# A Strassen-type MLP on one core: product sums kept across passes, and a quarter of the other two column blocks taken the same way

## The chip, the cores and the metric

One Trainium2 chip, one core of it. The metric is device time of one launch in microseconds (us); the kernel before takes 2032.7 us in the median of three runs (2032.12 to 2035.39). The engines named below are TensorE (PE in the profile, with PEld for its weight loads), VectorE (DVE), ScalarE (ACT), GpSimd (POOL) and SyncE (SP), whose queue issues nearly all transfers.

## The reference, cut to what matters

A decoder trunk of two layers over 256 tokens, model width 2048, hidden width 8192, in float32. Layer 0 mixes with a gated short convolution, layer 1 with multi-head latent attention; both end in the same kind of MLP, and the change is in the MLP.

```python
def sq_relu_mlp(x, w1, w2):
    return jnp.square(jax.nn.relu(x @ w1)) @ w2

for layer in range(DEPTH):
    ...
    h = layer_norm(ALPHA * h + mix, ln_g[layer, 0], ln_b[layer, 0])
    h = layer_norm(ALPHA * h + sq_relu_mlp(h, mlp_w1[layer], mlp_w2[layer]),
                   ln_g[layer, 1], ln_b[layer, 1])
```

## The kernel before, in words

**Precision.** TensorE multiplies operands of type float32r. To come near float32, every operand is split into a high part `hi` (a ScalarE cast, L116) and a low part `lo` (a VectorE subtraction, L117), and each product is made of three: hi·hi, hi·lo, lo·hi. So each weight tile of 128x1024 that arrives costs one cast of ScalarE and one subtraction of VectorE before TensorE can use it. `stream` (from L69) lists all weight tiles of 512 KB in the order in which TensorE wants them; `take` (L166) hands out the next and has later ones prepared, `LOOK` = 5 tiles ahead. Raw tiles have `RAW` = 5 buffers, split tiles `WA` = 8. Instructions are placed on their engines by a scheduler ahead of time, which may move an instruction of an engine before an earlier one that is not ready; on the chip each engine keeps its fixed order.

**The MLP** (`mlp`, L557) runs in `NQ` = 8 passes over the hidden width. A pass makes 8 tiles of 128 hidden units by 256 tokens (`products`, L265: 16 steps of one 512-wide and one 256-wide matmul each; `hidden`, L593: evacuation, ReLU, square, split into `h`), then multiplies them with the 1024 rows of W2 that belong to them, onto `acc`, 256 tokens by 2048, held in SBUF as 2 token tiles `t` by `NB` = 4 column blocks `n` of 512.

- `down` (L288), the plain way, takes one column block: 4 weight tiles, each of 2 K tiles by 512 columns, give 4 x 2 x 2 `dot`s. A `dot` (L274) is three matmuls with a 512-wide moving operand. That is 48 matmuls for a block.
- `down_fast` (L316), used in the six passes of `FAST` (1 to 6), takes blocks 0 and 1 together by a Strassen-Winograd step: 2 token tiles by 2 K tiles by 2 column blocks need 7 dots instead of 8, so 4 pairs of K tiles give 84 matmuls instead of 96. It needs seven PSUM banks ("4", "2", "3", "1", "6", "7", "5", in that order, `FACTORS` L313), sums of hidden tiles (`forms`, L602 to L609) and sums of weights, which `prepare` (L137 to L160) makes from two raw tiles: a difference of 1024 (L149), two of 512 (L152, L155), three splits of 1024 (`lo` twice, `lo_t`) and one of 512 (`t`, the operand "T4" of the first dot). The code counts such a unit as three tiles.
- `combine` (L642) adds the seven sums of a pass into `acc` right after: 11 additions of 128x512 on VectorE and one copy on ScalarE (L649), with a scratch `vu` from the pool of raw tiles. Blocks 2 and 3 then go through `down`, with four more additions.
- In the second MLP, `turn_residual` (L903) transposes the residual of one column block on TensorE and adds it to `acc`, in each of passes 1 to 4, between blocks 2 and 3.
- Pass 0 and pass 7 take all four blocks the plain way; pass 7 hands over to the norm behind it (`to_wide` L658, `to_out` L911). `to_out` loads gain and bias, `gbt`, on POOL's queue (L914).

**PSUM** has 8 banks, in two pools of four; `psum` (L180) counts its calls, and `Banks.next` (L106) gives calls 0 to 3 of each eight to one pool and 4 to 7 to the other.

Of the kernel before, what the change touches and what calls it, by code (L numbers as in the profile page):

```python
# [36 lines left out]
FAST = range(1, NQ - 1)  # L37
FIRST = (0, 1, 2, 4, 6, 8, 12, 16)
# [12 lines left out]
def trunk(ctx: ExitStack, tc: tile.TileContext, xT, vecs, w_first, w_in, w_out, w_kv, w_q, w_uk, w_uv,  # L51
          w_qn, w_qp, w_o, w1, w2, w2f, cosT, sinT, mask, ident, gb, out):
# [258 lines left out]


# [3 lines left out]
    def down_fast(x, forms):  # L316

        ps = {p: psum(f"ps_f{p}") for p, _, _ in FACTORS}
        n = len(x) // 2
        for j in range(n):  # L320
            b, = take(1)
            a = {"11": held(x[2 * j], 0), "12": held(x[2 * j + 1], 0), "22": held(x[2 * j + 1], 1)}
            for i in range(4):
                a[f"S{i + 1}"] = [forms[:, j, o, i * P:(i + 1) * P] for o in range(2)]
            for p, l, r in FACTORS:
                dot(ps[p], b[r], a[l], j == 0, j == n - 1)
        return ps
# [14 lines left out]
    cos_t = const.tile([P, T], F32, name="cos_t")  # L342
    sin_t = const.tile([P, T], F32, name="sin_t")
    mask_t = const.tile([P, 3 * P], F32, name="mask_t")
# [9 lines left out]

    def late_constants():
        nc.sync.dma_start(id_t, ident)
        nc.sync.dma_start(cos_t, cosT)
        nc.sync.dma_start(sin_t, sinT)
        nc.sync.dma_start(mask_t, mask)
# [193 lines left out]
    late_constants()  # L553
# [3 lines left out]
    def mlp(idx, ln, blocks, fast, begin=None, extra=None):  # L557
# [24 lines left out]

        for q in range(NQ):
# [8 lines left out]

            def hidden(m, ps, evac, *func):  # L593
                f = tmp.tile([P, T], F32, tag="fh", name="fh", bufs=3)
                evac(ps, f, *func)
                if not func:
                    nc.scalar.activation(f, f, AF.Relu)  # L597
                nc.scalar.activation(f, f, AF.Square)
                put_split(h[m], f)
                pair.append(f)  # L600
                if forms is not None and m % 2:
                    (a11, a21), (a12, a22) = ((v[:, :P], v[:, P:]) for v in pair[-2:])  # L602
# [39 lines left out]
    def combine(put, p):  # L642

        put(0, 1, p["4"])
        put(0, 0, p["2"])
        put(1, 0, p["3"])
        v, u = (raws.tile([P, 2, BW], F32, tag="raw", name="vu")[:, i, :] for i in range(2))
        put(0, 0, p["1"])
        nc.scalar.copy(v, p["1"])  # L649
        nc.vector.tensor_tensor(v, v, p["6"], ALU.add)  # L650
        nc.vector.tensor_tensor(u, v, p["7"], ALU.add)
        put(1, 0, v)
        put(0, 1, u)
        put(1, 0, p["5"])
        put(1, 1, u)
        put(1, 1, p["5"])
# [31 lines left out]
    with tc.tile_pool(name="att", bufs=1) as ap:  # L688
        lat = act.tile([P, 2 * NK, 2 * T], F32R, tag="c", name="lat")
        chl, qhl = ([lat[:, k, :] for k in range(o, o + NK)] for o in (0, NK))  # L690
        kpe = ap.tile([P, 2, T], F32, name="kpe")
# [6 lines left out]
        def rope(dst, src, rows):  # L698

            a = tmp.tile([P, T], F32, tag="sq", name="ropea")  # L700
            b = tmp.tile([P, T], F32, tag="nu", name="ropeb")
# [201 lines left out]
    def turn_residual(block, n):  # L903
        if 0 <= n < NB:
            for t in range(2):
                ps = psum("turned")
                for j in range(4):
                    nc.tensor.transpose(ps[:, j * P:(j + 1) * P], xres[:, 4 * n + j, t * P:(t + 1) * P], id_t)
                nc.vector.scalar_tensor_tensor(block(n, t), ps, ALPHA, block(n, t), ALU.mult, ALU.add)

    def to_out(block, put, h):  # L911
        gbt = act.tile([P, NB, 2 * BW], F32, tag="b", name="gbt")
        for n in range(NB):
            nc.gpsimd.dma_start(gbt[:, n, :], gb[n].partition_broadcast(P))  # L914
# [148 lines left out]
```

## Time and profile before

| | before |
|---|---|
| median of 3 runs | 2032.7 us (2032.12 to 2035.39) |
| the profiled execution: its time, its span | 2031.86 us, 2030.0 us |
| granted TensorE clock | 1.000 |
| busy: PE, PEld, DVE, ACT | 2022.8, 1763.4, 1637.1, 1186.2 us |
| the six passes of `FAST` in the first MLP | 455.4 to 970.1 us, 85.8 us each |
| in the second MLP | 1413.9 to 1932.2 us, 86.7 us each in passes 1 to 4, 85.8 us in 5 and 6 |

The profile is one execution. "PE" are matmuls, and as they are pipelined the duration of one is longer than the time from its start to the next one's; a cost per matmul is therefore read from starts. "Idle before" an instruction is time in which its engine did nothing, and the name behind the arrow is what ended it.

### The profile page before, as it was taken

To read this page: it belongs to the slowest core of one execution; us is meant where nothing else is said; L and a number is where in the kernel's file an instruction comes from. 1 tells how busy PE (TensorE), PEld (TensorE's weight loads), DVE (VectorE), ACT (ScalarE), POOL (GpSimd) and SP (SyncE) were. 2 spreads that over 40 slices of the span, in tenths; PEclk is the share of its full clock that TensorE was granted. 3 is DMA by queue.
4 is the path that set the end of the run, shared out by engine and by line. 5 is a ranking of instruction groups with operands and counts; after the bars stand their busy time and mean duration, and the time that the engine had idled before them with its cause. 6 is when DMAs were issued, how large, how long until landed. Compare 5 with 4: busy or idle time off the path is not lost.

```text
span 2030.0 us, 30192 instructions
## 1 busy us (share of the span) xinstructions
PE 2022.8 (100%) x11240; PEld 1763.4 (87%) x11240; DVE 1637.1 (81%) x2559; ACT 1186.2 (58%) x1849; POOL 4.5 (0%) x25
## 2 busy tenths in 40 slices
PE   9999999999999999999999999999999999999998
PEld 8888888988888888888889998898888888888886
DVE  7667677778898988989788978776889898898966
ACT  6444445676566565655656655566656656565661
POOL 0000000000000000000000000000000000000000
PEclk9999999999999999999999999999999999999999
DMA  8666666564746557465654544656474664746573
GB/s 307 209 191 187 188 190 193 162 210 138 251 148 216 193 170 256 145 229 174 232 176 153 177 129 137 195 168 205 136 240 155 213 204 164 250 143 221 190 228 121
DMA packets 106851, 385.32 MB, mean 190 GB/s; under 512 B 11856, under 2 KB 12752, under 8 KB 106448
## 3 DMA queue, kind: packets, MB, share of 16 engines
q1 hardware_dynamic: 105984, 381.17, 57.9%
q0 software_dynamic: 576, 2.10, 0.3%
q8 instruction: 88, 1.44, 0.3%
q14 instruction: 59, 0.48, 0.1%
q10 hardware_dynamic: 144, 0.13, 0.0%
HBM read 381.25 MB, written 2.10 MB: 189 GB/s over the span
## 4 chain that ended last, share of the span: by engine, by line
PE 99%; DMA 0%; DVE 0%; issue 0%; SPq 0%; ACT 0%; DVEq 0%
PE ps_u L192 20%; PE ps_l L192 13%; PE ps_u L196 11%; PE ps_d L276 7%; PE ps_d L277 7%; PE ps_d L278 7%; PE ps_l L196 7%; PE ps_f L278 4%; PE ps_f L276 4%; PE ps_f L277 4%; PE ps_w L226 1%; PE ps_w L224 1%; PE ps_w L225 1%; PE ps_g L226 1%; PE ps_g L224 1%; PE ps_g L225 1%
## 5 line engine op out<-in xcount | busy, mean ns | idle before, releaser
L117 DVE TENSOR_TENSOR lo<-raw,hi 128x1024 fp32r<-128x1024 f32 x710 | 858.7, 1222 | 271.5 <-ACT hi L116 199.9
L116 ACT CAST hi<-raw 128x1024 fp32r<-128x1024 f32 x710 | 740.9, 1050 | 428.4 <-DMA raw<-in_w_dram 134.6
L192 PE MATMUL ps_u<-xhl,hi 128*128 128x512 f32 x1792 | 621.3, 391 | 0.0
L196 PE MATMUL ps_u<-xhl,lo 128*128 128x256 f32 x1792 | 500.1, 280 | 0.0
L192 PEld LDWEIGHTS ps_u<-xhl,hi 128*128 128x128 f32 x1792 | 334.4, 187 | 71.9
L196 PEld LDWEIGHTS ps_u<-xhl,lo 128*128 128x128 f32 x1792 | 339.2, 189 | 1.7
L276 PE MATMUL ps_d<-hi,h 128*128 128x512 f32 x640 | 249.9, 390 | 0.0
L277 PE MATMUL ps_d<-lo,h 128*128 128x512 f32 x640 | 249.3, 390 | 0.0
L278 PE MATMUL ps_d<-hi,h 128*128 128x512 f32 x640 | 249.2, 389 | 0.0
L192 PE MATMUL ps_l<-xhl_a,hi 128*128 128x512 f32 x704 | 244.1, 393 | 0.0
L196 PE MATMUL ps_l<-xhl_a,lo 128*128 128x256 f32 x704 | 195.5, 280 | 0.0
L192 PEld LDWEIGHTS ps_l<-xhl_a,hi 128*128 128x128 f32 x704 | 132.2, 188 | 29.8
L278 PEld LDWEIGHTS ps_d<-hi,h 128*128 128x128 f32 x640 | 120.2, 188 | 25.2
L276 PEld LDWEIGHTS ps_d<-hi,h 128*128 128x128 f32 x640 | 120.2, 188 | 25.0
L277 PEld LDWEIGHTS ps_d<-lo,h 128*128 128x128 f32 x640 | 120.2, 188 | 24.6
L196 PEld LDWEIGHTS ps_l<-xhl_a,lo 128*128 128x128 f32 x704 | 131.9, 188 | 0.2
L597 ACT ACTIVATE fh<-fh 128x256 f32<-128x256 f32 x112 | 46.5, 415 | 89.2 <-DVE fh L333 89.1
L116 ACT CAST hi_t<-raw_t 128x1024 fp32r<-128x1024 f32 x48 | 50.6, 1054 | 55.5 <-DVE raw_t L149 30.5
L192 PE MATMUL ps_l<-z,hi 128*128 128x512 f32 x240 | 82.4, 391 | 0.0
L226 PE MATMUL ps_w<-xd,hi 128*128 128x258 f32 x256 | 72.7, 285 | 0.0
L224 PE MATMUL ps_w<-xd,hi 128*128 128x258 f32 x256 | 72.6, 284 | 0.0
L225 PE MATMUL ps_w<-xd,lo 128*128 128x258 f32 x256 | 72.4, 283 | 0.0
(253 smaller groups left out, 3185.1 us busy)
## 6 DMA issues: line engine op xcount, KB each, us to landing
raw<-in_w_dram SPq DMA_DIRECT2D x416, 512.0 KB, 4.3
raw<-in_w2f_dram SPq DMA_DIRECT2D x96, 512.0 KB, 3.5
raw<-in_w_in_dram SPq DMA_DIRECT2D x88, 512.0 KB, 3.8
raw<-in_w_out_dram SPq DMA_DIRECT2D x32, 512.0 KB, 3.6
raw<-in_w_o_dram SPq DMA_DIRECT2D x32, 512.0 KB, 4.0
raw<-in_w_kv_dram SPq DMA_DIRECT2D x10, 512.0 KB, 3.6
raw<-in_w_q_dram SPq DMA_DIRECT2D x8, 512.0 KB, 4.4
raw<-in_w_uk_dram SPq DMA_DIRECT2D x8, 512.0 KB, 4.6
```

The costliest lines, as they stand in the source:

```text
L116: nc.scalar.copy(hi, src)
L117: nc.vector.tensor_tensor(lo, src, hi.bitcast(F32), ALU.subtract)
L192: nc.tensor.matmul(ps, w[blk // 8][0][:, blk % 8, :], x, start=first, stop=False)
L196: nc.tensor.matmul(ps[:, :T], w[blk // 8][1][:, blk % 8, :], x[:, :T], start=False, stop=last)
L224: nc.tensor.matmul(ps[:, :W], hi, x[k][:, :W], start=k == 0, stop=False)
L225: nc.tensor.matmul(ps[:, :W], lo, x[k][:, :W], start=False, stop=False)
L226: nc.tensor.matmul(ps[:, :W], hi, x[k][:, W:], start=False, stop=k == NC - 1)
L276: nc.tensor.matmul(ps, x[0], w[0], start=first, stop=False)
L277: nc.tensor.matmul(ps, x[0], w[1], start=False, stop=False)
L278: nc.tensor.matmul(ps, x[1], w[0], start=False, stop=last)
L597: nc.scalar.activation(f, f, AF.Relu)
```

## The change

Four things in the MLP, and some moves that make room for them in SBUF.

1. `combine` goes. The seven sums of a pass are added to running sums (`keep`): "2", "3", "4", which go to one place each, straight to `acc`; "1", "6", "7", "5" to `sums`, 16 KB a partition. In pass 1 the first visit to `sums` is a copy on ScalarE.
2. `fold` brings `sums` into `acc` once an MLP, eight additions of 128x1024 on VectorE, one after each hidden tile of pass 7.
3. Blocks 2 and 3 are taken together (`down_pairs`). Three of the four pairs of K tiles are multiplied the plain way, onto four banks named "22", "3", "2", "4"; the fourth goes through the seven dots, of which "4", "2", "3" continue on the banks of that name and "1", "6", "7", "5" get new ones. `turn_residual` is called twice with one token tile each.
4. `hidden` works on two tiles of a pair in one buffer, and splits both with one cast and one subtraction of 128x512.
5. Room: `cos_t`, `sin_t`, `mask_t` are loaded at the start of the attention; `ropeb` shares a buffer; `gbt` is loaded on SP's queue, and the scratch of POOL's queue is cut to 4096.

```diff
+PLAIN = QC // 2 - 1
...
-            lead = 0
-            if q in FAST:
-                out += [(w2f[l, q, j, 0], w2f[l, q, j, 1]) for j in range(QC // 2)]
-                lead = 2
-            out += halves(w2[l, q, lead:])
+            if q not in FAST:
+                out += halves(w2[l, q])
+                continue
+            out += [(w2f[l, q, j, 0], w2f[l, q, j, 1]) for j in range(QC // 2)]
+            for j in range(PLAIN):
+                out += halves(w2[l, q, 3, j]) + halves(w2[l, q, 2, j])
+            out += [(w2g[l, q, j, 0], w2g[l, q, j, 1]) for j in range(QC // 2 - PLAIN)]
...
-    def down_fast(x, forms):
-
-        ps = {p: psum(f"ps_f{p}") for p, _, _ in FACTORS}
-        n = len(x) // 2
-        for j in range(n):
-            b, = take(1)
...
-                dot(ps[p], b[r], a[l], j == 0, j == n - 1)
-        return ps
+    OWN = ("1", "6", "7", "5")
+    def fast_products(ps, x, forms, j, fresh, last):
+
+        b, = take(1)
...
+            dot(ps[p], b[r], a[l], p in fresh, last)
...
+        sums = fast.tile([P, 4, 2, BW], F32, name=f"sums{idx}")
+
+        def keep(p, g, ps):
+
+            at = sums[:, OWN.index(p), g, :] if p in OWN else \
+                block(*{"2": (2 * g, 0), "3": (2 * g + 1, 0), "4": (2 * g, 1), "22": (2 * g + 1, 1)}[p])
+            if q == 1 and p in OWN:
+                nc.scalar.copy(at, ps)
+            else:
+                nc.vector.tensor_tensor(at, at, ps, ALU.add)
+
+        def down_pairs(h, forms):
+
+            n = QC // 2
+            ps = {p: psum(f"ps_f{p}") for p, _, _ in FACTORS}
+            for j in range(n):
+                fast_products(ps, h, forms, j, ps if j == 0 else (), j == n - 1)
+            for p in ps:
+                keep(p, 0, ps[p])
+            ps = {p: psum("ps_d") for p in ("22", "3", "2", "4")}
+            for j in range(PLAIN):
+                for nb, two in ((3, ((1, "22"), (0, "3"))), (2, ((0, "2"), (1, "4")))):
+                    w, = take(1)
+                    for t, p in two:
+                        for kk in range(2):
+                            k = 2 * j + kk
+                            dot(ps[p], wide_rows(w, kk), held(h[k], t), k == 0, p == "22" and k == 2 * PLAIN - 1)
+                if extra and q <= NB and j < 2:
+                    extra(block, q - 1, j)
+            keep("22", 1, ps["22"])
+            for p in OWN:
+                ps[p] = psum(f"ps_f{p}")
+            for j in range(PLAIN, n):
+                fast_products(ps, h, forms, j, OWN if j == PLAIN else (), j == n - 1)
+            for p in ("3", "2", "4", *OWN):
+                keep(p, 1, ps[p])
+
+        def fold():
+
+            s1, s6, s7, s5 = (sums[:, i] for i in range(4))
+            c = acc.rearrange("p t (g b c) -> p t b g c", g=2, b=2)
+            for d, a, b in ((c[:, 0, 0], c[:, 0, 0], s1), (s6, s6, s1), (c[:, 0, 1], c[:, 0, 1], s6), (s7, s7, s6),
+                            (c[:, 1, 0], c[:, 1, 0], s7), (c[:, 1, 1], c[:, 1, 1], s7),
+                            (c[:, 0, 1], c[:, 0, 1], s5), (c[:, 1, 1], c[:, 1, 1], s5)):
+                nc.vector.tensor_tensor(d, a, b, ALU.add)
+                yield
...
             def hidden(m, ps, evac, *func):
-                f = tmp.tile([P, T], F32, tag="fh", name="fh", bufs=3)
+                both = pair_tile(m) if forms is not None else None
+                f = both[:, m % 2, :] if forms is not None else tmp.tile([P, T], F32, tag="fh", name="fh", bufs=3)
...
-                put_split(h[m], f)
-                pair.append(f)
-                if forms is not None and m % 2:
+                if forms is None:
+                    put_split(h[m], f)
+                elif m % 2:
+                    at = ht[:, m - 1:m + 1, :]
+                    split(at[:, :, :T], at[:, :, T:], both)
...
+                folds = fold()
                 for m, ps in enumerate(products(QC, xhl, turned=None if q == NQ - 1 and begin else TURNED)):
                     hidden(m, ps, whole)
+                    if q == NQ - 1:
+                        next(folds)
...
             if q in FAST:
-                combine(put, down_fast(h, forms))
-            for n in range(2 if q in FAST else 0, NB):
-                if n == NB - 1 and extra:
-                    extra(block, q - 1)
-                down(h, put, n)
+                down_pairs(h, forms)
+            else:
+                for n in range(NB):
+                    down(h, put, n)
...
-            nc.gpsimd.dma_start(gbt[:, n, :], gb[n].partition_broadcast(P))
+            nc.sync.dma_start(gbt[:, n, :], gb[n].partition_broadcast(P))
```

More of the change, by code (lines that the diff above doesn't have):

```diff
@@ L552, in trunk @@
                 ln.prepare(k)
-    late_constants()
+    nc.sync.dma_start(id_t, ident)
     ln.widen("a1", "a2")
@@ L598, in hidden @@
                 nc.scalar.activation(f, f, AF.Square)
-                put_split(h[m], f)
-                pair.append(f)
-                if forms is not None and m % 2:
-                    (a11, a21), (a12, a22) = ((v[:, :P], v[:, P:]) for v in pair[-2:])
+                if forms is None:
[3 more added lines that the diff above has]
+                    split(at[:, :, :T], at[:, :, T:], both)
+                    (a11, a21), (a12, a22) = ((both[:, i, :P], both[:, i, P:]) for i in range(2))
                     sf = fast.tile([P, 4, P], F32, tag="sf", name="sf")
@@ L690, in trunk @@
         chl, qhl = ([lat[:, k, :] for k in range(o, o + NK)] for o in (0, NK))
+        cos_t = ap.tile([P, T], F32, name="cos_t")
+        sin_t = ap.tile([P, T], F32, name="sin_t")
+        mask_t = ap.tile([P, 3 * P], F32, name="mask_t")
+        for t, source in ((cos_t, cosT), (sin_t, sinT), (mask_t, mask)):
+            nc.sync.dma_start(t, source)
         kpe = ap.tile([P, 2, T], F32, name="kpe")
@@ L700, in rope @@
             a = tmp.tile([P, T], F32, tag="sq", name="ropea")
[L701 removed]
+            b = tmp.tile([P, T], F32, tag="evac", name="ropeb")
             nc.vector.tensor_tensor(a[rows], src[rows], cos_t[rows], ALU.mult)
@@ L900, in trunk, with turn_residual @@
     summed(after, out_chunks(), residual)
[L903 to L909, printed above, removed]
+    def turn_residual(block, n, t):
+        ps = psum("turned")
+        for j in range(4):
+            nc.tensor.transpose(ps[:, j * P:(j + 1) * P], xres[:, 4 * n + j, t * P:(t + 1) * P], id_t)
+        nc.vector.scalar_tensor_tensor(block(n, t), ps, ALPHA, block(n, t), ALU.mult, ALU.add)
     def to_out(block, put, h):
@@ L1043 @@
         "w2f": np.stack([np.stack([_pairs(q[:, :2 * BW]) for q in w.reshape(NQ, QC * P, D)]) for w in a["mlp_w2"]]),
+        "w2g": np.stack([np.stack([_pairs(q[2 * PLAIN * P:, 2 * BW:]) for q in w.reshape(NQ, QC * P, D)])
+                         for w in a["mlp_w2"]]),
         "cosT": np.tile(cos, (4, 1)),
```

40 lines of the change are left out of this document (12 added, 28 removed).

## The prediction

> **What bounds the kernel now.** I read the page first: busy time by engine, then the chain of work that ended last.
>
> ```profile
> span 2030.0 us, 30192 instructions
> PE 2022.8 (100%) x11240; PEld 1763.4 (87%) x11240; DVE 1637.1 (81%) x2559; ACT 1186.2 (58%) x1849; POOL 4.5 (0%) x25
> ...
> PE 99%; DMA 0%; DVE 0%; issue 0%; SPq 0%; ACT 0%; DVEq 0%
> ```
>
> TensorE runs almost without a gap and is 99% of the chain. Such a kernel gains only by fewer or shorter matmuls, and loses where something makes TensorE wait. So I look at one pass of `FAST` (pass 2 of the first MLP), cut at the first matmul of each stage. The timeline of TensorE gives the cuts (start, duration, line, operands):
>
> ```profile
> 540.25 0.39 PE L192 MATMUL ps_u<-xhl,hi 128*128 128x512 f32 x1
> ...
> 584.64 0.39 PE L276 MATMUL ps_f<-t,h 128*128 128x512 f32 x1
> ...
> 599.33 0.40 PE L276 MATMUL ps_f<-t,h 128*128 128x512 f32 x1
> ...
> 604.23 0.40 PE L276 MATMUL ps_d<-hi,h 128*128 128x512 f32 x1
> ...
> 626.03 0.39 PE L192 MATMUL ps_u<-xhl,hi 128*128 128x512 f32 x1
> ```
>
> The hidden products take 44.39 us, the 84 seven-dot matmuls 19.59, the 96 plain ones 21.80: 85.78 in all. Now the busy time in these stretches, the products halved (stretch; length; PE; PEld; DVE; ACT; POOL; clock; DMA share; GB/s):
>
> ```profile
> 540.25:562.00 21.75, 21.75 (x127) 19.18 (x126) 16.20 (x23) 13.65 (x22) 0.00 (x0) 1.00 0.72 236
> 562.00:584.64 22.64, 22.64 (x132) 20.00 (x131) 21.16 (x37) 15.23 (x28) 0.00 (x0) 1.00 0.34 100
> 584.64:604.23 19.59, 19.59 (x86) 15.78 (x85) 18.18 (x24) 12.67 (x18) 0.00 (x0) 1.00 0.59 191
> 604.23:626.03 21.80, 21.80 (x98) 18.03 (x96) 19.16 (x23) 10.73 (x12) 0.00 (x0) 1.00 0.76 260
> ...
> sum 85.78, PE 85.78 PEld 72.98 DVE 74.69 ACT 52.28 POOL 0.00; mean PE 85.78 PEld 72.98 DVE 74.69 ACT 52.28 POOL 0.00
> ```
>
> TensorE never waits, at full clock. VectorE is the second: idle for 11.09 us of the pass, nearly full from 562 to 604. There its margin is thin: the fourth seven-dot unit's last-made operand, "T4" (`t`), is read at 599.33, and the timeline of VectorE has it finished at 598.00 + 0.68 = 598.68, 0.65 us before.
>
> ```profile
> 598.00 0.68 DVE L117 TENSOR_TENSOR t<-raw,t 128x512 fp32r<-128x512 f32 x1
> ...
> 604.97 0.68 DVE L581 TENSOR_TENSOR acc<-acc,ps_f 128x512 f32<-128x512 f32 x1
> 605.56 1.22 DVE L117 TENSOR_TENSOR lo<-raw,hi 128x1024 fp32r<-128x1024 f32 x1
> ...
> 613.21 1.22 DVE L117 TENSOR_TENSOR lo<-raw,hi 128x1024 fp32r<-128x1024 f32 x1
> ```
>
> **TensorE's part.** Each of the 12 passes loses two plain weight tiles, 24 matmuls, and gains one seven-dot unit, 21. A plain matmul costs 21.80 / 96 = 0.2271 us, one of the seven-dot kind 19.59 / 84 = 0.2332. So 24 x 0.2271 - 21 x 0.2332 = 5.45 - 4.90 = 0.55 us a pass, 6.6 us in 12. I take each kind at its own price; if the new dots ran at the plain price it would be 3 x 0.2271 x 12 = 8.2 us, the lower bound.
>
> The Trainium skill, in "TensorE: Matmul & The Clock Gate", section "Wait — 56ns, not 53.3ns?", gives one price for every warm matmul of 512 columns, 215.7 ns from start to start. This trace has two, both dearer, and the measured ones decide; by the page's figure the saving would be 36 x 0.2157 = 7.8 us, an estimate inside my bounds, and the sum below 2025.1.
>
> **Split transposes.** In passes 1 to 4 of the second MLP one run of eight transposes becomes two runs of four. TensorE's timeline around such a run:
>
> ```profile
> 1487.87 1.03 PE L908 MATMUL turned<-id_t,xres 128*128 128x128 f32 x8
> 1488.66 0.48 PE L276 MATMUL ps_d<-hi,h 128*128 128x512 f32 x1
> 1488.97 0.40 PE L277 MATMUL ps_d<-lo,h 128*128 128x512 f32 x1
> ```
>
> The run costs 0.79 us, and the first matmul behind it 0.31 instead of 0.23, so leaving and entering a run costs about 0.1 us. One more such seam in four passes: between 0 and 0.8 us; I take 0.4.
>
> **VectorE's part.** The groups of VectorE in the pass (count; busy, mean ns; idle before):
>
> ```profile
> L117 DVE TENSOR_TENSOR lo<-raw,hi 128x1024 fp32r<-128x1024 f32 x32 | 38.4, 1222 | 8.6 <-ACT hi L116 8.5
> L149 DVE TENSOR_TENSOR raw_t<-raw,raw 128x1024 f32<-128x1024 f32 x4 | 4.9, 1222 | 0.3 <-DMA raw<-in_w2f_dram 0.3
> L117 DVE TENSOR_TENSOR lo_t<-raw_t,hi_t 128x1024 fp32r<-128x1024 f32 x4 | 4.9, 1218 | 0.0
> L581 DVE TENSOR_TENSOR acc<-acc,ps_f 128x512 f32<-128x512 f32 x6 | 4.0, 683 | 0.0
> ...
> L338 DVE TENSOR_TENSOR h<-fh,h 128x256 fp32r<-128x256 f32 x8 | 3.4, 420 | 0.0
> ...
> L155 DVE TENSOR_TENSOR raw<-raw 128x512 f32<-128x512 f32 x4 | 2.8, 690 | 0.1
> L152 DVE TENSOR_TENSOR raw<-raw,raw_t 128x512 f32<-128x512 f32 x4 | 2.7, 687 | 0.0
> L117 DVE TENSOR_TENSOR forms<-sf,forms 128x512 fp32r<-128x512 f32 x4 | 2.7, 686 | 0.0
> L117 DVE TENSOR_TENSOR t<-raw,t 128x512 fp32r<-128x512 f32 x4 | 2.7, 683 | 0.0
> ```
>
> - Removed: two plain splits, 2 x 1.222 = 2.44 us.
> - Added: the unit's seven, 2 x 1.222 + 1.222 + 1.218 + 0.687 + 0.690 + 0.683 = 6.94.
> - Paired hidden split: 4 x 0.686 for 8 x 0.420, -0.62.
> - PSUM sums: 11 + 4 before, 7 + 8 after, all of 128x512: nothing. In pass 1 eight go to ScalarE, which is busy for 52 of 86 us.
>
> That is +3.9 us, or +3.8 as neighbours overlap (604.97 to 605.56 is 0.59 for an instruction of 0.68). VectorE's 74.7 becomes 78.5 of a pass of 85.2, idle 6.7. `combine`'s copy on ScalarE and VectorE's wait for it go.
>
> It is hidden if the 3.8 us fall where VectorE has room, and are worked off before 562. In the last stretch, from 604.23 on, `combine` occupies VectorE: between 606.78 (605.56 + 1.22) and 613.21 it splits no weight tile. Now five sums stand there ("3", "1", "6", "7", "5", 5 x 0.6 = 3.0), so the next split may come 3.4 us earlier, and of the plain blocks' sums two fewer stand in the stretch, 1.2 us; the new unit costs 6.9 - 2.4 = 4.5 more. So the next pass starts about level. The seven sums of the fourth pair fall at its start, five more than now, 3 us, into a stretch with 21.75 - 16.20 = 5.55 idle. From 562 on, where the 0.65 us margin is made, nothing is added. I take 0 for this term. With no cover it is the 3.8 us a pass of rival 3.
>
> What VectorE waits for, and the queue of SP in the last stretch (waited for; us in total, times, longest):
>
> ```profile
> ACT hi L116 <- PE ps_u L192: 6.1, 7, 1.7
> ...
> SPq L127 <- DVE acc L581: 5.0, 2, 3.6
> ```
>
> ScalarE's casts, which VectorE follows, wait 6.1 us for buffers that TensorE still reads: that is spare time. And SP waited 5.0 us for `combine` to give its raw tile back; with `vu` gone, weights come earlier. Bytes per pass are the same, 32 tiles.
>
> **The moved and the single edits.** `fold`: eight additions of 128x1024, 1.222 each, 9.8 us in pass 7, in whose 45 us of products VectorE splits no seven-dot unit; nothing. `gbt` on SP's queue is the one moved wait. Its four issues on POOL, SP's last weight issues, and VectorE's first use of `gbt`, from the three timelines, and a weight tile's landing from the page's list of issues:
>
> ```profile
> 1976.11 2.23 POOL L914 DMA_DIRECT2D gbt<-in_gb_dram  x4 [1032.21 <-PE ps_u L196]
> ...
> 1925.73 60.96 SPq L127 DMA_DIRECT2D raw<-in_w_dram  x26
> ...
> 1989.77 0.69 DVE L931 TENSOR_TENSOR acc<-acc,gbt 128x512 f32<-128x512 f32 x1
> ...
> raw<-in_w_dram SPq DMA_DIRECT2D x416, 512.0 KB, 4.3
> ```
>
> The four need the buffer of the hidden products' operand, free at 1976.1, and the last weight tiles now stand behind them. SP issues its last weight tile at 1986.7, when TensorE has 43 us of plain matmuls from 1976 on; at most 8 split and 5 raw tiles are ahead, 2.7 us of work each. Held up to 1976.1 plus four issues of about half a microsecond, SP delays nothing that is due before 1990; first use of `gbt` is 1989.77. Nothing, bounded by 2 us. The rope constants, 448 KB in three transfers, go on the same queue at the attention's start, five tiles of the latent products before their use: nothing; uncovered it is one landing, 4.3 us.
>
> **Banks.** This is a new wait. With two transposes between, ten banks are drawn from eight in a pass. Counting calls from the opening of the second MLP's banks (13 + 3 + 2 + 5 + 8 = 31 up to pass 1), "5" in passes 2, 3 and 4 falls to a pool whose four banks hold two or three of "3", "2", "4" and the new ones, so it must wait for one to be emptied. The dots run "4", "2", "3", "1", "6", "7", "5" at 0.70 us each: "3" ends at 2.1 us, "5" starts at 4.2. An emptying takes 0.68. If VectorE is free, 1.4 us are left over; if weight splits stand before it (1.22 each, two or three) "5" waits 1 to 2 us, and all work of TensorE behind it. Bound 0 to 6 us over three passes; I take 0.6.
>
> **Sum.** 2031.9 (the profiled execution, 0.8 below the median of 2032.7) - 6.6 + 0.4 + 0.6 = 2026.3. I forecast 2026.5.
>
> **Rivals.**
> 1. *T4 comes late.* VectorE reaches 562 behind by a debt D, and TensorE waits D - 0.65 at the fourth unit of every pass. For it: VectorE has one idle stretch a pass and the change uses half of it. Against: the 6.1 us above. With D = 2 us: 12 x 1.35 = 16 us, 2043. From 0.9 us of waiting a pass the kernel is slower than 2036.8.
> 2. *The bank wait is real.* Splits stand before the emptying of "3": 6 us in place of 0.6, 2032, no change. For it: in the rows above a sum of a bank done by 601 is added only at 604.97, as splits go first.
> 3. *VectorE sets the pass.* If its 11.1 us idle are all waits that stay, a pass takes 78.5 + 11.1 = 89.6, 3.8 more than now: 2031.9 + 46 = 2077. The spare 6.1 us speak against it. The Trainium skill, "Perfetto Trace Analysis", section "Identifying the Most-Contended Engine", judges VectorE by occupancy and TensorE by its weight loads: after the change 92% against 85%, so VectorE would set the time; before it, DVE's 74.69 already passed PEld's 72.98 and TensorE did not wait.
> 4. *The saving is smaller than it says.* If the 72 plain matmuls left also run at 0.2332, 72 x 0.0061 x 12 = 5.3 us are lost: 2031.6. For it: nothing tells what makes the two prices. Against: they stay one stretch of plain dots.
>
> **How the numbers follow.** A measurement of this kernel can tell about 0.2% from no change, 4.1 us: under 2028.6 is faster, over 2036.8 slower. Forecast 0.52 (2023.5 to 2028.5), rival 1 0.20, rival 2 0.16, rival 3 0.05, rival 4 0.07. Faster 0.52; the same 0.23; slower 0.25. The range goes from the lower bound, 2031.9 - 8.2 = 2023.7, to rival 1's 2043; left out are rival 3, the far part of rival 1 (0.10) and a little below (0.03).
>
> **What would show it.** Right: 84 + 21 matmuls of `ps_f` and 72 of `ps_d` in a pass of 85.2 us, no wait of TensorE over 0.3 us in the passes, DVE at 78 to 79 us. Wrong: TensorE waiting at L276 for `t` (rival 1) or for a sum of VectorE on a bank (rival 2); plain dots of 0.233 (rival 4); a pass longer than 85.8.

## The result, and the profile after

The changed kernel takes 2040.8 us (median of 6 runs, 2038.11 to 2043.0) beside 2031.98 of the kernel before (6 runs): ratio 1.004, 95% interval 1.0027 to 1.0053. It is slower, by 8.8 us; forecast was 2026.5, faster. The profiled execution took 2041.59. From the page of the changed kernel:

```profile
span 2039.4 us, 30080 instructions
...
PE 2027.7 (99%) x11204; PEld 1754.9 (86%) x11204; DVE 1685.0 (83%) x2571; ACT 1196.3 (59%) x1829; POOL 2.3 (0%) x21
...
PE 92%; DVE 4%; DMA 2%; issue 1%; ACT 1%; SPq 0%; ACTq 0%; DVEq 0%
```

And its view of what TensorE waits for (us in total, times, longest):

```profile
PE ps_u L195 <- DVE acc L584: 2.3, 3, 1.2
...
PE ps_f L279 <- DVE acc L584: 1.1, 2, 0.6
...
PE ps_d L279 <- DVE acc L584: 0.6, 2, 0.4
```

The 36 matmuls are gone (11240 to 11204), and yet TensorE is busy for 4.9 us more: some matmuls became dearer. And the chain leaves TensorE for 8% of its way: it goes through VectorE's work, and the casts and transfers ahead of that, from places where TensorE waits for a sum that VectorE adds late. So there are two costs. The first shows in one pass without a wait, pass 3 of the first MLP, cut as in the prediction: hidden products, seven-dot stage, plain stage (with 9 matmuls of the new unit, whose first three dots write its banks), rest of the new unit.

```profile
625.68:670.89 45.21, 45.21 (x257) 39.23 (x256) 40.88 (x60) 29.36 (x46) 0.00 (x0) 1.00 0.55 182
670.89:690.39 19.50, 19.50 (x87) 15.83 (x85) 17.54 (x23) 12.72 (x17) 0.00 (x0) 1.00 0.63 191
690.39:708.86 18.47, 18.47 (x83) 15.21 (x81) 18.08 (x21) 8.65 (x10) 0.00 (x0) 1.00 0.64 208
708.86:711.65 2.79, 2.79 (x13) 2.25 (x12) 1.69 (x3) 2.19 (x3) 0.00 (x0) 1.00 1.02 417
sum 85.97, PE 85.97 PEld 72.52 DVE 78.19 ACT 52.92 POOL 0.00; mean PE 21.49 PEld 18.13 DVE 19.55 ACT 13.23 POOL 0.00
```

The last two rows make 21.26 us where the plain stage took 21.80: 0.54 saved, as forecast. But the hidden products, which the change does not touch, take 45.21 instead of 44.39, 0.82 more, without any wait and at full clock. The timeline of TensorE shows how, here four matmuls of the kernel before (start, duration):

```profile
544.08 0.39 PE L192 MATMUL ps_u<-xhl,hi 128*128 128x512 f32 x1
544.31 0.28 PE L196 MATMUL ps_u<-xhl,lo 128*128 128x256 f32 x1
544.43 0.39 PE L192 MATMUL ps_u<-xhl,hi 128*128 128x512 f32 x1
544.66 0.28 PE L196 MATMUL ps_u<-xhl,lo 128*128 128x256 f32 x1
```

And four of the changed kernel, in the same view:

```profile
544.64 0.40 PE L195 MATMUL ps_u<-xhl,hi 128*128 128x512 f32 x1
544.89 0.28 PE L199 MATMUL ps_u<-xhl,lo 128*128 128x256 f32 x1
545.01 0.40 PE L195 MATMUL ps_u<-xhl,hi 128*128 128x512 f32 x1
545.24 0.28 PE L199 MATMUL ps_u<-xhl,lo 128*128 128x256 f32 x1
```

From one wide matmul to the next it is 0.35 us before; after, 0.37 here and 0.35 at the pairs beside it. Over 128 pairs it is 44.39 / 128 = 346.8 ns against 45.21 / 128 = 353.2. The second cost is waiting. It stands in some passes only. Four of them, whole, by the windows of the changed kernel:

```profile
883.58:972.25 88.67, 87.14 (x436) 72.56 (x435) 79.97 (x107) 54.39 (x77) 0.00 (x0) 1.00 0.59 197
1502.73:1590.55 87.82, 87.23 (x442) 73.11 (x441) 75.54 (x100) 53.38 (x77) 0.00 (x0) 1.00 0.58 186
1590.55:1678.60 88.05, 87.04 (x442) 72.57 (x441) 79.09 (x107) 53.11 (x75) 0.00 (x0) 1.00 0.59 192
1678.60:1766.58 87.98, 87.45 (x443) 73.07 (x441) 79.38 (x107) 52.60 (x75) 0.00 (x0) 1.00 0.58 190
```

The first is pass 6 of the first MLP, 2.70 us longer than the 85.97 above (0.24 of it are two matmuls for the norm that the kernel before has here too). The other three are passes 2 to 4 of the second MLP; with some 0.95 us of transposes each would be 86.9, and they are about 1 us longer. Here is the place in pass 2, on TensorE's timeline in the changed kernel:

```profile
1588.76 0.40 PE L281 MATMUL ps_f<-hi_t,forms 128*128 128x512 f32 x1
1589.75 0.51 PE L279 MATMUL ps_f<-hi_t,forms 128*128 128x512 f32 x1 [0.59 <-DVE acc L584]
...
1591.48 0.50 PE L195 MATMUL ps_u<-xhl,hi 128*128 128x512 f32 x1 [0.53 <-DVE acc L584]
```

And on VectorE's:

```profile
1585.52 1.22 DVE L120 TENSOR_TENSOR lo<-raw,hi 128x1024 fp32r<-128x1024 f32 x1
1587.87 1.22 DVE L120 TENSOR_TENSOR lo<-raw,hi 128x1024 fp32r<-128x1024 f32 x1 [1.13 <-ACT hi L119]
1589.01 0.68 DVE L584 TENSOR_TENSOR acc<-acc,ps_d 128x512 f32<-128x512 f32 x1
1589.61 1.22 DVE L120 TENSOR_TENSOR lo<-raw,hi 128x1024 fp32r<-128x1024 f32 x1
```

Dot "5" needs a bank that is emptied at 1589.01 + 0.68 = 1589.69, and starts at 1589.75. The sum stood in VectorE's queue behind a weight split, which itself waited 1.13 us for ScalarE's cast.

The account of the span, from such rows of all passes: saved 12 x 0.54 in the plain stage and 0.09 in each of six seven-dot stages (19.50 for 19.59), 7.0 us; products +0.82 in ten passes and +0.73 in pass 7 of the first MLP, 8.9; waits 7.5. That gives +9.4, and the span grew by 2039.4 - 2030.0 = 9.4. Two passes need a word. Pass 3 of the second MLP has products of 45.20 us too, but behind the wait at their start its pairs are 346.7 ns apart, the fast spacing: its 0.8 is a wait. And in pass 7 of the first MLP the products became slow behind a wait of 1.25 us.

### The profile page after: what moved, and what is told of

Read it like the earlier page. It is cut to its first block, busy times and chain, and to the rows that moved or that the text cites. A ratio compares the mean times of both kernels' runs of the same rounds, so it can differ in the third digit from the quotient of the medians.

```text
span 2039.4 us, 30080 instructions
## 1 busy us (share of the span) xinstructions
PE 2027.7 (99%) x11204; PEld 1754.9 (86%) x11204; DVE 1685.0 (83%) x2571; ACT 1196.3 (59%) x1829; POOL 2.3 (0%) x21
## 4 chain that ended last, share of the span: by engine, by line
PE 92%; DVE 4%; DMA 2%; issue 1%; ACT 1%; SPq 0%; ACTq 0%; DVEq 0%
PE ps_u L195 20%; PE ps_l L195 13%; PE ps_u L199 10%; PE ps_l L199 7%; PE ps_d L279 6%; PE ps_d L281 6%; PE ps_d L280 6%; PE ps_f L279 3%; PE ps_f L281 3%; PE ps_f L280 3%; DMA raw<-in_w_dram 2%; PE ps_w L229 1%; PE ps_w L227 1%; PE ps_w L228 1%; DVE lo L120 1%
## 5 line engine op out<-in xcount | busy, mean ns | idle before, releaser
L195 PE MATMUL ps_u<-xhl,hi 128*128 128x512 f32 x1792 | 630.6, 397 | 2.3 <-DVE acc L584 2.3
L279 PE MATMUL ps_d<-hi,h 128*128 128x512 f32 x556 | 218.0, 392 | 0.7 <-DVE acc L584 0.6
L281 PE MATMUL ps_d<-hi,h 128*128 128x512 f32 x556 | 216.8, 390 | 0.0
L280 PE MATMUL ps_d<-lo,h 128*128 128x512 f32 x556 | 216.7, 390 | 0.0
L279 PEld LDWEIGHTS ps_d<-hi,h 128*128 128x128 f32 x556 | 104.4, 188 | 24.4 <-DVE acc L584 1.5
L281 PEld LDWEIGHTS ps_d<-hi,h 128*128 128x128 f32 x556 | 104.4, 188 | 22.1
L280 PEld LDWEIGHTS ps_d<-lo,h 128*128 128x128 f32 x556 | 104.4, 188 | 21.5
L119 ACT CAST hi_t<-raw_t 128x1024 fp32r<-128x1024 f32 x60 | 62.9, 1049 | 79.8 <-DVE raw_t L152 64.7
L645 ACT ACTIVATE fp<-fp 128x256 f32<-128x256 f32 x96 | 40.0, 417 | 103.1 <-DVE fp L334 103.1
L152 DVE TENSOR_TENSOR raw_t<-raw,raw 128x1024 f32<-128x1024 f32 x60 | 73.1, 1218 | 6.8 <-DMA raw<-in_w2f_dram 6.5
L120 DVE TENSOR_TENSOR lo_t<-raw_t,hi_t 128x1024 fp32r<-128x1024 f32 x60 | 73.2, 1221 | 1.3
L229 PE MATMUL ps_w<-xd,hi 128*128 128x258 f32 x256 | 72.7, 285 | 0.0
```

What stands on the lines that cost most here:

```text
L119: nc.scalar.copy(hi, src)
L120: nc.vector.tensor_tensor(lo, src, hi.bitcast(F32), ALU.subtract)
L152: nc.vector.tensor_tensor(t.rearrange(two, a=2), b12.unsqueeze(1).to_broadcast([P, 2, BW]), r1.rearrange(two, a=2), ALU.subtract)
L195: nc.tensor.matmul(ps, w[blk // 8][0][:, blk % 8, :], x, start=first, stop=False)
L229: nc.tensor.matmul(ps[:, :W], hi, x[k][:, W:], start=False, stop=k == NC - 1)
L279: nc.tensor.matmul(ps, x[0], w[0], start=first, stop=False)
```

## The experiments

The letters in the expectations are the theories. A: the products are slow because seven-dot matmuls run right before them, whatever else the change does; A1: the exchange of low before high at step 2 of the first product (`TURNED`), which suits plain dots as neighbours, does it. C: the waits come from VectorE's load. D: they come from the order in which VectorE takes sums and weight splits.

**e1_swap.** The kernel before, with nothing of the change but the place of the seven-dot stage: behind the plain blocks.

```diff
-            if q in FAST:
-                combine(put, down_fast(h, forms))
             for n in range(2 if q in FAST else 0, NB):
...
                 down(h, put, n)
+            if q in FAST:
+                combine(put, down_fast(h, forms))
```

> The kernel before, with the order inside the six passes turned round: blocks 2 and 3 the plain way first, then the 84 seven-dot matmuls, so that the next pass's hidden products follow seven-dot matmuls as they do in the changed kernel; nothing else of the change. Theory A (hidden products that follow seven-dot matmuls run slower, 45.21 us for 8 instead of 44.39, and stay so for the whole stage): products of passes 2 to 7 take 45.2 us in both MLPs, 12 x 0.82 = 9.8 us more, about 2042, if VectorE keeps up. Theory B (the products are slower for another reason that came with the change: the paired hidden tiles, other buffers): products stay at 44.4 us, about 2032.

Measured: 2041.04 (2040.54 to 2041.35), ratio 1.0041 (1.0026 to 1.0056). Its windows of pass 2 (products, plain stage):

```profile
540.18:585.39 45.21, 45.21 (x257) 39.20 (x256) 38.22 (x59) 29.89 (x51) 0.00 (x0) 1.00 0.74 235
585.39:607.21 21.82, 21.82 (x98) 18.03 (x97) 20.06 (x28) 10.89 (x14) 0.00 (x0) 1.00 0.38 109
```

The same matmuls in another order, no wait, and the products take 45.21. A holds.

**g4_swapun.** The same, and the exchange left out in passes 2 to 7.

```diff
-products(QC, xhl, turned=None if q == NQ - 1 and begin else TURNED)
+products(QC, xhl, turned=TURNED if q == 1 else None)
```

> e1 (the kernel before with the seven-dot stage last in the pass) with the exchange left out in passes 2 to 7. Theory A1: products back from 45.2 to 44.4 us, time from 2041.0 to about 2031.5. Theory A2: 2041.

Measured: 2031.88 (10 runs), ratio 1.0001 (0.9992 to 1.0011). Its window of the products of pass 2:

```profile
540.45:584.84 44.39, 44.39 (x258) 39.13 (x256) 38.08 (x58) 29.88 (x50) 0.00 (x0) 1.00 0.76 239
```

One exchange of two matmuls at the start sets the spacing of all 256 behind it, and with it 9.2 us of the kernel. A1 is shown for the kernel before. In the changed kernel the exchange stands ahead of the ten passes with slow products; pass 7 of the first MLP has it in none of these kernels, so the slow products there come from something else.

**e5_unturned.** The same exchange left out, in the changed kernel.

> The changed kernel, with the exchange of the 512-wide and the 256-wide matmul at step 2 of the first hidden product (turned=TURNED) left out in passes 2 to 7, whose products follow seven-dot matmuls; pass 1, which follows plain ones, keeps it. Theory A1 (the two widths can run in two phases, 346.8 or 353.2 ns a pair; what ran before decides the phase a stage starts in, the exchange flips it, and the stage keeps it): without the exchange the products take 44.4 us, and the time falls by 10 us to about 2031. Theory A2 (after seven-dot matmuls the products are slow whatever their order): 45.2 us, 2040.8.

Measured: 2043.76 (2038.25 to 2046.44), ratio 1.0057 (1.0037 to 1.0076): nothing won. Products of pass 2, and the seven-dot stage of pass 3, by its windows:

```profile
540.10:584.48 44.38, 44.38 (x257) 39.12 (x256) 36.35 (x54) 29.07 (x48) 0.00 (x0) 1.00 0.54 165
669.74:691.25 21.51, 20.32 (x87) 15.64 (x86) 19.93 (x27) 13.12 (x20) 0.00 (x0) 1.00 0.62 169
```

And one of its waits of TensorE:

```profile
PE ps_f L280 <- DVE t L120: 1.8, 5, 0.6
```

The products are fast again, but for two passes behind waits: pass 7 of the first MLP (45.31) and pass 5 of the second (45.21). And TensorE now waits for what the slow products had given VectorE time for: T4 (`t`), 21.51 where 19.59 was, and banks.

**e3_banks** takes the bank wait alone: after the split transposes the count of banks is set back (`Banks.count -= 2`), so that "5" gets another bank.

> The changed kernel with the count of PSUM calls set back by the two transposes alone, so that 'the four new banks fall two to each pool and need no bank of a live sum. Theory A and B alike: products stay at 45.2 us. If the gaps of 0.6 to 0.8 us ahead of dot 5 and ahead of the next products in passes 2 to 4 of the second MLP are the overdrawn pool, they go: about 2037.5. If they are VectorE being late with every sum, they stay or move: 2040.

Measured: 2040.88 (2037.56 to 2043.95), ratio 1.0041 (1.0028 to 1.0053). In its profile, that of its fastest execution (span 2035.4), the waits at "5" and at the start of the products are gone from passes 2 to 4 of the second MLP, which take 86.91, 86.91 and 87.40 us; the median over all runs is the changed kernel's all the same.

**e2_last** puts the new unit ahead of the last pair of plain tiles, so that plain dots stand before the products, and sets the count back.

> The changed kernel with the new seven-dot unit moved ahead of the last plain pair, so that 24 plain matmuls stand between it and the next pass's products, and with the count of PSUM calls set back by the two transposes so that no pool of banks is overdrawn. Theory A: products back at 44.4 us, and the bank waits gone: 2040.8 - 9.8 - 3.5 = about 2027.5. Theory B: products stay at 45.2 us, about 2037. If the operands of the unit are late now (it comes 5.4 us earlier in the pass), gaps at the first dot of the unit, and up to 2035.

Measured: 2047.69 (2043.96 to 2050.32), ratio 1.0073 (1.0058 to 1.0088). The unit's operands are wanted earlier: waits for `t` in nine places, 5.6 us, and for banks before the products, 6.6. The products, behind plain dots and with the exchange, are at 44.39 where nothing holds up their start. Held up, they can turn slow: in pass 4 of the first MLP by 0.04 us only, as the last plain matmul and the first of the products on TensorE's timeline are 0.27 us apart instead of 0.23, and the stage takes 45.30:

```profile
712.64 0.39 PE L282 MATMUL ps_d<-hi,h 128*128 128x512 f32 x1
712.91 0.47 PE L196 MATMUL ps_u<-xhl,hi 128*128 128x512 f32 x1
```

**e4_plain** keeps the sums from pass to pass, but leaves blocks 2 and 3 wholly plain (`PLAIN = QC // 2`); no new unit, VectorE's work less than in the kernel before.

> The changed kernel with blocks 2 and 3 wholly plain (four of four pairs): sums kept and folded, paired hidden tiles, moved transfers, but no new seven-dot unit. Theory A: products follow plain matmuls, 44.4 us; VectorE does less than before: 2032, give or take 1. Theory B: 45.2 us, about 2042. If keeping and folding cost something themselves, the time lies above 2033 with products at 44.4.

Measured: 2035.69 (10 runs), ratio 1.0021 (1.0011 to 1.003): with 96 plain matmuls and products of 44.39 there are waits still, by the starts of the matmuls some 3.7 us in eight passes. Its window of pass 4 of the first MLP, beside 85.78 before:

```profile
712.24:798.26 86.02, 86.02 (x438) 72.90 (x437) 71.96 (x96) 51.48 (x72) 0.00 (x0) 1.00 0.61 196
```

VectorE has only 71.96 us here. That speaks against load as the cause, and for order. What the change did to the plain stage can be read in the code: `down` drew two banks for 48 matmuls, 10.9 us; `down_pairs` draws four banks at once and writes all four within the first 24 matmuls, 5.5 us. So the sums that empty the banks of the seven-dot stage are due much earlier than before.

**g1_pool, g3_all.** Less load for VectorE: the four sums S1 to S4 on GpSimd (`nc.gpsimd.tensor_tensor`), exchange left out, banks set back; g3_all with the layout of g2_forms besides.

> The changed kernel with the exchange left out in passes 2 to 7 (as e5), the bank count set back (as e3), and the four sums of hidden tiles S1 to S4 moved from VectorE to GpSimd: 16 instructions of 0.286 us a pass, 4.6 us less for VectorE, less than it had before the change. Theory C (the waits of TensorE for T4 and for banks come from VectorE having no room left): the waits go, products stay at 44.4 us, a pass takes 85.2 us, and the time is 2026 to 2028. Theory D (they come from the order in which sums and splits stand on VectorE, or from the transfers, not from its load): waits of the same size as in e5, about 2040. If GpSimd slows VectorE, the mean of its instructions grows.

> g1 with the layout of g2. If both do what they are meant to: 2020 to 2023. If the layout does nothing, as g1.

Measured: 2097.37, ratio 1.0324 (1.0309 to 1.0339), and 2098.91, 1.033 (1.0313 to 1.0348). Two groups of g1_pool (busy, mean ns):

```profile
L657 POOL TENSOR_TENSOR sf<-fp 128x128 f32<-128x128 f32 x48 | 56.8, 1183 | 221.9 <-ACT fp L648 221.9
...
L120 DVE TENSOR_TENSOR h<-fp,h 128x512 fp32r<-128x512 f32 x48 | 45.6, 950 | 0.0
```

An addition of 0.28 us on VectorE takes up to 1.18 on GpSimd, and VectorE's own instruction beside it went from 0.684 to 0.950 us. TensorE waited 26.7 us for T4, 26 times, and 14.8 us for T4's cast. Of C and D these runs tell nothing.

**f1_h, f2_w, f3_b, g2_forms** ask why seven-dot matmuls cost 0.2332 (rival 4). All are the kernel before. f1_h takes blocks of `h` where the forms S1 to S4 were the stationary operand; f2_w takes the moving operands from plain weight tiles; f3_b puts the seven dots on two banks (these three compute something else); g2_forms lays the forms out differently.

> The kernel before, with hidden tiles h in place of the sums 'forms' as the stationary operand of dots 3, 6, 7 and 5, so it computes something else. It asks what makes a seven-dot matmul 0.2332 us and a plain one 0.2271. If it is the tile 'forms' as weights: the 84 matmuls take 19.1 us. If not: 19.6.

> The kernel before, with the halves of the two plain split tiles as the moving operand of every dot, in place of T1 to T4, so it computes something else. If the made-up weight tiles are what costs: the 84 matmuls take 19.1 us. If not: 19.6.

> The kernel before, with the seven dots on two PSUM banks in turn in place of seven, so it computes something else. If the change of bank among seven is what costs (plain dots change between two): the 84 matmuls take 19.1 us. If not: 19.6.

> The kernel before with the sums of hidden tiles laid out as the hidden tiles are, high and low part 1 KB apart in place of 2 KB. If the distance is what makes the tile forms dear as weights: 84 seven-dot matmuls in 19.2 us as in f1, 12 x 0.4 = 4.7 us less, about 2027. If it is another tile, whatever its layout, between two of h: 19.6 us and 2032.

Measured, in single runs: 2026.78, 2031.13 and 2033.39; g2_forms 2031.84, ratio 1.0 (0.9991 to 1.001). The window of the seven-dot stage of f1_h:

```profile
584.26:603.45 19.19, 19.19 (x86) 15.78 (x85) 18.18 (x25) 12.02 (x17) 0.00 (x0) 1.00 0.61 194
```

19.19 / 84 = 0.2285 against 0.2332; f2_w had 19.52, f3_b and g2_forms 19.59. Most of the extra price comes with the forms as stationary operand, not from the moving operands, banks or layout. What it is about the forms stays open.

**h2_base, h1_less, h4_order** tell C from D. Base: the changed kernel, exchange left out, banks set back. h1_less: VectorE's additions to the kept sums "1", "6", "7", "5" left out from pass 2 on, so a part of the down projection is missing. h4_order: the same work as the base, but at the last seven-dot unit and at the new unit weights are split only two tiles ahead instead of five, so that the sums stand in VectorE's queue before the splits:

```diff
-            if ahead > LOOK:
+            if ahead > state.get("look", LOOK):
...
+                state["look"] = LOOK if j < n - 1 else 2
                 fast_products(ps, h, forms, j, ps if j == 0 else (), j == n - 1)
...
+            state["look"] = LOOK
...
+                state["look"] = 2
                 fast_products(ps, h, forms, j, OWN if j == PLAIN else (), j == n - 1)
+                state["look"] = LOOK
```

> The changed kernel with the exchange of the first product left out in passes 2 to 7 and the bank count set back by two after the split transposes. Products 44.39 us in every pass where TensorE did not wait just before them, a pass without waits 85.1 us. If nothing waited: 2031.9 - 6.5 = about 2026. Both theories of the stalls expect waits again: VectorE has 78 us of work in an 85.1 us pass. C (its load) and D (the order in which it takes sums and weight splits) expect 2034 to 2043, with TensorE waiting on weight tiles (T4) in the seven-dot stage and on sums (banks) in the plain stage.

> As the kernel beside it, with the additions that keep the seven dots' own sums of products 1, 6, 7 and 5 left out in passes 2 and later (their earlier value stays, so part of the down projection is missing): VectorE some 4.8 us less in each pass, 73.4 instead of 78.2, below the 74.7 of the kernel before. C (load): the waits on weight tiles and banks go, pass 85.1 to 85.3, 2025 to 2029. D (order): the splits still stand before the sums of the plain stage, its bank waits of 0.2 to 0.9 us stay in half of the passes, 2032 to 2043.

> As the first kernel, with the look-ahead of the weight splits cut to two tiles at the last seven-dot unit and at the new unit, so that VectorE takes the sums before the next splits. D: the bank waits of the plain stage go, and unless the tiles then come late, 2027 to 2031. C: the same work, only in another order; the wait moves to the weight tiles, 2034 to 2043.

Measured: h2_base 2039.57 (2036.51 to 2045.4), ratio 1.0037 (1.0026 to 1.0048); h1_less 2028.25 (2026.83 to 2031.49), 0.9982 (0.9973 to 0.999); h4_order 2027.32 (2025.63 to 2028.4), 0.9975 (0.9964 to 0.9985). VectorE's timeline at the end of the seven-dot stage in pass 3 of h2_base:

```profile
688.15 1.23 DVE L120 TENSOR_TENSOR lo<-raw,hi 128x1024 fp32r<-128x1024 f32 x1 [0.20 <-ACT hi L119]
689.29 0.68 DVE L584 TENSOR_TENSOR acc<-acc,ps_f 128x512 f32<-128x512 f32 x1
691.83 1.23 DVE L120 TENSOR_TENSOR lo<-raw,hi 128x1024 fp32r<-128x1024 f32 x1 [1.86 <-ACT hi L119]
692.98 0.68 DVE L584 TENSOR_TENSOR acc<-acc,ps_f 128x512 f32<-128x512 f32 x1
```

TensorE's, there:

```profile
693.81 0.47 PE L279 MATMUL ps_d<-hi,h 128*128 128x512 f32 x1 [0.40 <-DVE acc L584]
```

And the window of that pass:

```profile
625.99:712.76 86.77, 86.06 (x435) 72.12 (x434) 78.22 (x105) 52.81 (x75) 0.00 (x0) 1.00 0.59 195
```

VectorE's timeline at the same place of h4_order:

```profile
684.40 2.35 DVE L120 TENSOR_TENSOR lo<-raw,hi 128x1024 fp32r<-128x1024 f32 x2
686.67 1.88 DVE L584 TENSOR_TENSOR acc<-acc,ps_f 128x512 f32<-128x512 f32 x3
688.47 2.47 DVE L584 TENSOR_TENSOR sums<-sums,ps_f 128x512 f32<-128x512 f32 x4
690.86 5.76 DVE L120 TENSOR_TENSOR lo<-raw,hi 128x1024 fp32r<-128x1024 f32 x5
```

And its window of the pass:

```profile
625.16:710.56 85.40, 85.40 (x435) 72.30 (x434) 78.21 (x106) 53.31 (x75) 0.00 (x0) 1.00 0.63 199
```

VectorE's work is the same, 78.22 and 78.21 us in the pass; the pass is 1.37 us shorter. In h2_base VectorE stands idle for 1.86 us before a split whose cast is not done, with a sum behind it in its queue that could run; TensorE's 13th plain matmul, the first for the third bank, then waits for that sum. So with equal work the order alone makes the waits come or go: D is shown so far. But what D expected of h1_less, waits that stay (2032 to 2043), did not come; 2028.25 is what C expected. VectorE's timeline of h1_less at that place:

```profile
689.24 1.23 DVE L120 TENSOR_TENSOR lo<-raw,hi 128x1024 fp32r<-128x1024 f32 x1 [1.37 <-ACT hi L119]
690.38 0.68 DVE L584 TENSOR_TENSOR acc<-acc,ps_f 128x512 f32<-128x512 f32 x1
```

The sum stands behind the unready split as in h2_base, but with less work ahead of it VectorE ends it at 691.06, and the 13th plain matmul starts at 691.33 without a wait. The waits thus need both, sums behind splits and a VectorE that is late; either can be taken away, and the load need not fall. By the weight-load side of the Trainium skill's rule on occupancy ("Perfetto Trace Analysis", section "Identifying the Most-Contended Engine") VectorE, at 78.21 against 72.30 of weight loads, would still be the most contended engine; in this pass of h4_order TensorE doesn't wait for it, and takes 85.40 us where the same work took 86.77.

**h3_half** has the new unit in passes 2, 4 and 6 only, in the old order.

> The new unit of seven dots only in passes 2, 4 and 6 of each MLP, all blocks of the other two plain in passes 1, 3, 5 and 7, sums still kept; the exchange of the first product left out behind a pass with the new unit. Saving 0.55 us in 6 passes, 3.3 us; VectorE 72 us in a pass without the unit, so that it catches up. C: 2028.5 to 2031, faster than before; D: bank waits in the passes without the unit too (as in the kernel with both blocks plain), 2032 to 2037.

Measured: 2036.55 (2034.72 to 2039.06), ratio 1.0022 (1.0014 to 1.0031). That is what D expected: reserve in every other pass is not enough in the old order.

**i1_turned, i2_banks.** i1_turned is h4_order with the exchange as the change has it. i2_banks is h4_order with the bank count as the change has it, which makes it the changed kernel with the look-ahead and the exchange altered, nothing else.

> The changed kernel with the look-ahead cut in the plain stage and the bank count set back, its exchange of the first product kept as the change has it. Order theory and product theory together: no waits of size, but products at 45.21 us again in passes 2 to 7, so 0.82 x 11 + 0.73 = 9.8 us over the kernel with the exchange left out (2027.3): 2036 to 2038. Were the stalls only gone because the products were fast, it stays at about 2040.8, the changed kernel's time; if the order alone had made the products fast, about 2027.

> The kernel with the look-ahead cut and the exchange left out, but the bank count left as the change has it: only the wait of dot 5 on its bank in the second MLP comes back. The prediction's term says 0.6 us in all, so 2027.9; its rival 2 says 0.5 us in each of 10 to 12 passes, 2032 to 2033; the gaps of the changed kernel's profile, 0.4 to 1.0 us in passes 2 to 4 of the second MLP, say up to 3.6 us, 2028 to 2031, unless sums that stand before the splits let the bank go earlier.

Measured: i1_turned 2033.89 (2033.31 to 2035.22), ratio 1.0009 (1.0 to 1.0018); i2_banks 2025.9 (2025.24 to 2027.7), ratio 0.997 (0.9959 to 0.9982): the fastest of all, and faster than the kernel before. i1_turned has the products at 45.21 in eleven passes, here those of pass 2 by the windows, and between TensorE's matmuls no gap of a wait over 0.3 us in any pass:

```profile
539.89:585.10 45.21, 45.21 (x257) 39.19 (x256) 37.29 (x54) 28.95 (x48) 0.00 (x0) 1.00 0.49 161
```

It came 2 us under its expectation, which had left out that the seven-dot stage behind slow products is 0.09 us shorter in ten passes (0.9 us in all), that h4_order still had some short waits for T4, and that pass 7 of the first MLP, without a wait ahead of it, takes 44.57 as in the kernel before, so that its 0.73 does not come. The page of i2_banks:

```profile
span 2024.0 us, 30084 instructions
...
PE 2016.5 (100%) x11204; PEld 1754.6 (87%) x11204; DVE 1685.1 (83%) x2571; ACT 1196.6 (59%) x1829; POOL 2.3 (0%) x21
```

And its window of pass 2 of the first MLP:

```profile
539.74:624.97 85.23, 85.23 (x435) 72.35 (x433) 76.09 (x103) 54.04 (x78) 0.00 (x0) 1.00 0.60 199
```

The two causes side by side, medians in us (in brackets: with the bank count set back):

| | sums behind splits | sums before splits |
|---|---|---|
| exchange kept | 2040.8 (2040.88) | (2033.89) |
| exchange left out | 2043.76 (2039.57) | 2025.9 (2027.32) |

They do not add. Fast products win 8.0 us where nothing waits (2033.89 to 2025.9; by the rows 9.0 of products less 0.9 of seven-dot stages), or 6.6 with the banks alike (2033.89 to 2027.32, which has the short waits for T4), and nothing that can be told where sums stand late; the better order wins 7.0 with slow products (2040.88 to 2033.89) and 12.3 with fast ones (2039.57 to 2027.32).

## Why the prediction was wrong

- **TensorE's part, 0.55 us a pass: right.** 0.54 in the changed kernel, 85.78 - 85.23 = 0.55 in i2_banks. Plain dots stayed at their price, and the new dots cost that of the seven-dot kind.
- **What the sum did not hold: the products.** It took 6.6 from 2031.9 and left all other matmuls at their measured price. This is the step that failed first: the change put seven-dot matmuls where plain dots had stood before the products, and the 256 matmuls that follow went from 44.39 to 45.21 us in ten passes, 8.2 us in all, more than the 7.0 saved (shown by e1_swap and g4_swapun); 0.73 came on top in pass 7 of the first MLP, behind a wait. Rival 4 had the doubt, "nothing tells what makes the two prices", and turned it on the plain dots, the wrong stage; its 2031.6 did not come. The one price that the Trainium skill gives for a warm matmul of 512 columns ("TensorE: Matmul & The Clock Gate", section "Wait — 56ns, not 53.3ns?") leaves no room for this: one sequence of matmuls runs at 346.8 or 353.2 ns a pair here, and the measurement decides.
- **VectorE's part: its size right, its cover wrong.** 78.5 us a pass was forecast, 78.19 measured. "I take 0 for this term" failed by order: the prediction counted how much VectorE does in a stretch, not which instruction it has at the head of its queue. It also read the plain stage as one of the same banks, and did not see that four are wanted within 24 matmuls. With the waits outside the three passes of the bank term, this cost about 3.7 us here, and far more once the products are fast (h2_base against h4_order, 12.3).
- **Banks, 0.6 us: mis-sized, inside its bound of 0 to 6.** 0.9, 1.9 and 0.95 us in passes 2 to 4, 3.7 in all; with the banks set back (e3_banks) 0.5 of it is left. Rival 2 described it (splits before the emptying), also with an old row as evidence. But i2_banks has the same ten banks of eight and no such wait over 0.3 us, so the transposes alone do not make it; the order does its part.
- **Split transposes, 0.4: about right.** By the windows, pass 2 of the second MLP took 86.69 before and 86.18 in i2_banks, a gain of 0.51 where passes without the seam gain 0.55: 0.04 a pass, 0.2 in all.
- **Rival 1, T4 late:** not in the changed kernel but for one wait in a late pass, as the slow products gave VectorE 0.8 us a pass. In e5_unturned and h2_base it came (3.2 us in nine waits in h2_base). **Rival 3** did not come: 85.97 and not 89.6. The fold, `gbt` on SP's queue and the rope constants left no wait that the profile names.
- **Sum.** With the two causes taken away, the prediction's own sum holds: 2026.3 worked out, 2025.79 in the profiled execution of i2_banks.

What makes TensorE keep one spacing or the other, and why the forms as stationary operand cost more, was not settled; behind delays of 0.04 and 1.25 us the slow one came, behind 1.14 in pass 7 of the first MLP of e3_banks the fast one, so the kind of neighbour alone does not set it. The shorter look-ahead of h4_order also moves casts and transfers; that the order of sums and splits is what counts is read from VectorE's rows, not tried apart. That drawing two banks at a time in the plain stage would also do away with the waits is argued from the place of the wait; it wasn't tried.

## What to carry to other kernels

A matmul that a change does not touch can change its price when its neighbour changes, so list what now runs right before each unchanged stage, and measure that stage by windows first. Where an engine works through its queue in order, ask not only how busy it is but what stands ahead of the one instruction that frees a bank: half a microsecond of work behind an unready split stalls TensorE while VectorE itself is idle. Two faults can hide each other, as here, where each alone seemed to win nothing or half; take them away together before the idea is given up.

## What was not expected of the hardware

- TensorE runs alternating matmuls of 512 and 256 columns at 346.8 or 353.2 ns a pair, at a granted clock of 1.0, and keeps for a whole stage the spacing with which it began; the same exchange of two matmuls gives the fast one behind plain dots and the slow one behind seven-dot matmuls, and a start held up by 0.04 us behind plain dots gave the slow one too (45.30 us, e2_last).
- Matmuls with the forms as stationary operand make a stage of 84 dearer, 19.59 against 19.19 us with `h` in their place; the layout of the forms in memory makes no difference (19.59).
- Additions of 128x128 on GpSimd took 0.54 to 1.18 us, on VectorE 0.28, and slowed an instruction of VectorE's beside them from 0.684 to 0.950 us.
